# Two RWKV chunks inverted together, with state steps and attention projections woven between them in a written-out TensorE order

## The chip, the cores and the metric

The kernel runs on one core of a Trainium2 chip. A core has TensorE for matrix products, VectorE, ScalarE, GpSimd, and SyncE, which issues transfers. The profile calls them PE (with PEld for the loads of TensorE's weights), DVE, ACT, POOL and SP. The metric is the device time of one execution, in microseconds (us). One execution was also profiled; all rows below are from that one.

## The reference

A trunk of two layers over 528 tokens (16 meta tokens and 512 others) of width 1024. Each layer normalises, makes one projection of 3488 columns, feeds three groups of heads with it (A: RWKV-7, B: differential attention, C: gated linear attention), joins them in an output projection, and ends with 16 experts that each take 66 tokens. What the change touches is group A's recurrence, and the projections of group B that are computed beside it.

```python
def step(S, inp):                       # group A, for each token, both directions
    r_t, w_t, k_t, v_t, kk_t, ka_t = inp
    sa = jnp.einsum("dbhvk,dbhk->dbhv", S, kk_t)
    S = S * w_t[..., None, :] - sa[..., :, None] * ka_t[..., None, :] + v_t[..., :, None] * k_t[..., None, :]
    return S, jnp.einsum("dbhvk,dbhk->dbhv", S, r_t)
...
p = jnp.einsum("bld,dp->blp", u, w_in[l])                 # u: 528 x 1024
q = rotary(q...) * (B_QK_DIM ** -0.5); k = rotary(k...)   # group B, 4 heads
```

## The kernel before

The 528 tokens are padded to nine chunks of 64. For each chunk the recurrence becomes matrix products and one inversion of a unit triangular 64x64 matrix for each of 8 combinations (two directions `d`, four heads; `m` from 0 to 3 counts direction and head pair, `p_` is the half of a pair: partitions 0 to 63 or 64 to 127, given by `hr(p_)`). Step `i` handles chunk `i` of the forward direction and chunk `8 - i` of the backward one.

One step of `rwkv` has two parts.

- **The inversion**, which doesn't need the running state `S`. `pl` (products of `BC` and `az`) is masked into `lt` by VectorE; ScalarE rounds `lt` to half precision (`nh`); VectorE makes `mt` and the first `tz` from it. Five levels follow, each `pq` (TensorE), `vv` (ScalarE), `pz` (TensorE), a subtraction into `tz` and a transpose of it (VectorE). Then `pzt`, `pF`, `pZ` refine the result into `zz`.
- **The state step**: `pbc` and `plv` prepare operands, then `px` from `S`, `xs` on VectorE, `pu` with `zz`, `uv` on ScalarE and VectorE, `pS` and the next `S`, and the output `py` into `Y`.

`az` and `zz` are copies of the operands laid into 128 rows, with zeros in the rows of the other half, so that one product of 128 rows serves both halves.

Ahead of the loop stands `prep`, which makes `AQ`, `BC` and `vt` mainly on VectorE. Behind it in the program stand `heads` (the 12 blocks of 128 columns of group B: projections `pj`, each 48 products of 128x128 weights with 264 columns, 24 for each half of the tokens; then rotary, or a transpose into `vB`), `fin` (normalises `Y`) and `attention` (scores `sm` and `S` at L894 and L904). The program text has the loop first and `heads` next. The order that each engine really gets is decided by the framework's scheduler when the kernel is built, and it mixes the products of `heads` with those of the loop. Engines run their own lists strictly in order and wait for each other by semaphores. `behind(inst, mark)` fixes that `inst` is issued after `mark`, without a wait. PSUM tiles: `rw0` and `rw1` (one each) for the inversion, `sm` (two) for the state step, `mm` (two) for projections.

Of the kernel before, what the change touches and what calls it, by code (L numbers as in the profile page):

```python
# [27 lines left out]
HL = L // 2  # L28
# [38 lines left out]
CST_COLS = _lay([("ident", 128), ("eye", 64), ("ones", 1), ("half", 2), ("ltmask", 512), ("base", 128),  # L67
# [3 lines left out]
def constants():  # L71
# [10 lines left out]
    put("ltmask", np.concatenate([s < t, s < t, s <= t, s <= t, s > t, s > t, s >= t, s >= t], 1))  # L82
# [23 lines left out]
def body(ctx: ExitStack, tc: tile.TileContext, a, out, dbg=None, depth=DEPTH, stop=None):  # L106
# [110 lines left out]
    for l in range(depth):  # L217
# [65 lines left out]
        def proj(blk, M=128):  # L283
            w = wp.tile([128, 1024], F32, name="w")
            nc.sync.dma_start(w, a["w_in"][l, blk])
            wh, wl = split(wp, w, 1024, 2, V if BLK_B <= blk < BLK_C else G)
            p = mm_tile("pj")
            vh = wh.rearrange("p (k m) -> p k m", k=KT)
            vl = wl.rearrange("p (k m) -> p k m", k=KT)
            for c in range(2):  # L290
                n = 0
                for ww, uu in ((vh, uh), (vh, ul), (vl, uh)):
                    for k in range(KT):
                        T.matmul(p[:M, c, :HL], ww[:, k, :M], uu[:, k, c * HL:(c + 1) * HL],  # L294
                                 start=(n == 0), stop=(n == 23))
                        n += 1
            return p[:M, :, :HL]

# [147 lines left out]
        def rwkv(rw):  # L446
            Y = rw.tile([128, 2, NCH, CH], F32, name="Y")
            S = rw.tile([128, 4, CH], F32, name="S", bufs=2)
            G.memset(S, 0.0)
            bc4 = [128, 4, CH]  # L450
            m4 = lambda x: x[:, :256].rearrange("p (m n) -> p m n", m=4)
            MP = [(m, p_) for m in range(4) for p_ in range(2)]
            eyeb = eye[:, None, :].to_broadcast(bc4)
            AZ = [rw.tile([128, 4, 2, 2, CH], F32, name=f"az{x}") for x in range(2)]
            ZZ = [rw.tile([128, 4, 2, CH], F32, name=f"zz{x}") for x in range(1)]
            for p_ in range(2):
                G.memset(ZZ[0][hr(1 - p_), :, p_, :], 0.0)
            for x in range(2):
                for p_ in range(2):
                    G.memset(AZ[x][hr(1 - p_), :, 0, p_, :], 0.0)  # L460
                    G.memset(AZ[x][hr(1 - p_), :, 1, 1 - p_, :], 0.0)
            for i in range(NCH):
                js = (i, NCH - 1 - i)
                jm = [js[m // 2] for m in range(4)]
                az, zz = AZ[i % 2], ZZ[0]
                for d in range(2):
                    for p_ in range(2):
                        for x in range(2):
                            src = AQ[hr(p_), 2 * d:2 * d + 2, js[d], x, :]
                            if x == 0:  # L470
                                A.activation(az[hr(p_), 2 * d:2 * d + 2, 0, p_, :], src, AF.Copy)
                            else:
                                G.tensor_copy(az[hr(p_), 2 * d:2 * d + 2, 1, 1 - p_, :], src)
                lt = rw.tile([128, 2, 512], F32, name="lt", bufs=2).rearrange("p d (b x q n) -> p d b x q n", b=2, x=2, q=2)
                for d in range(2):
                    pl = rw_tile(i, "pl").rearrange("p (b n) -> p b n", b=2)
                    for b in range(2):
                        m = 2 * d + b
                        T.matmul(pl[:, b, :], flat(BC[m][:, jm[m]]), az[:, m].rearrange("p x q n -> p (x q n)"),
                                 start=True, stop=True)  # L480
                    V.tensor_mul(lt[:, d].rearrange("p b x q n -> p b (x q n)"), pl,
                                 ltmask[:, d, None, :].to_broadcast([128, 2, 256]))
                nh = rw.tile(bc4, F16, name="nh", bufs=2)
                nl = rw.tile(bc4, F16, name="nl", bufs=2)
                db = lambda x: x.rearrange("p (d b) n -> p d b n", d=2)
                for p_ in range(2):
                    A.activation(db(nh[hr(p_)]), lt[hr(p_), :, :, 0, p_, :], AF.Copy)
                for p_ in range(2):
                    G.tensor_sub(db(nl[hr(p_)]), lt[hr(p_), :, :, 0, p_, :], db(nh[hr(p_)]))
                mt = rw.tile([128, 5, 4, CH], F16, name="mt", bufs=2)  # L490
                for d in range(2):
                    V.tensor_mul(mt[:, :, 2 * d:2 * d + 2, :],
                                 nh[:, None, 2 * d:2 * d + 2, :].to_broadcast([128, 5, 2, CH]),
                                 lvlm[:, :, d, None, :].to_broadcast([128, 5, 2, CH]))
                tz = rw.tile([128, 2, 4, CH], F16, name="tz", tag=f"tz{i % 2}", bufs=2)
                V.tensor_mul(tz[:, 1].rearrange("p (d b) n -> p d b n", d=2),
                             nh.rearrange("p (d b) n -> p d b n", d=2),
                             basem[:, :, None, :].to_broadcast([128, 2, 2, CH]))
                V.tensor_sub(tz[:, 1], eyeb, tz[:, 1])
# [898 lines left out]
```

## Time and profile before

| | |
|---|---|
| median of three runs | 2705.39 us (2701.43 to 2705.64) |
| profiled execution, its own time | 2698.94 us |
| its span, first to last instruction | 2697.2 us |
| TensorE busy | 2513.8 us (93%) |
| VectorE busy | 2158.7 us (80%) |
| ScalarE busy | 1608.8 us (60%) |
| GpSimd busy | 351.8 us (13%) |
| mean granted TensorE clock, share of full speed | 0.951 |

The two layers run one after the other. The loop of the first layer lies at about 250 to 430 us, that of the second at about 1585 to 1765 us. Each is followed by attention, the output projection and the experts; the experts fill most of the span. A busy TensorE is not a TensorE at its peak: a product's row shows its whole passage through the array, and rows of successive products overlap. The step from the start of one product to the start of the next is what it costs.

### The profile page before, as it was taken

Reading aid. Unit: us, or ns where it says so; the run is one execution under the profiler, and the core shown is the slowest. Engines: PE = TensorE matmul, PEld = TensorE weight load, DVE = VectorE, ACT = ScalarE, POOL = GpSimd, SP = SyncE. Lnnn points to the kernel's source line nnn. Section 1 sums busy time; section 2 is a strip of 40 time slices with the busy share of each in tenths; the row PEclk is TensorE's granted clock in tenths of the full one; section 3 lists DMA queues with packets and bytes.
Section 4 is the critical chain, followed back from the end, with each engine's and each line's share of the span. In section 5 each row is a group of like instructions: output and inputs, shape, how many; then the busy total and the mean of one; then the engine's idle time right before and its main releaser. Section 6 shows DMA issues by size and latency. Waiting matters only on the chain. (4 is left out here: it accounts for less than half of the span.)

```text
span 2697.2 us, 46680 instructions
## 1 busy us (share of the span) xinstructions
PE 2513.8 (93%) x18586; PEld 1983.7 (74%) x18586; DVE 2158.7 (80%) x3389; ACT 1608.8 (60%) x2113; POOL 351.8 (13%) x503
## 2 busy tenths in 40 slices
PE   7889999887999999999788899999699999999995
PEld 6778886666777777778587787756478777777783
DVE  3557677768999999999735666776699999999995
ACT  4324335526888888888542343354178888888884
POOL 3113321001000000000121133210010000000000
PEclk9887999998999999999988889999899999999998
DMA  3101101158999999999420111022499999999993
GB/s 131 48 25 58 39 25 48 64 211 319 403 407 398 410 398 411 399 414 411 174 85 32 40 45 49 14 75 101 150 394 397 411 398 410 400 407 401 413 412 114
DMA packets 84683, 643.30 MB, mean 239 GB/s; under 512 B 12592, under 2 KB 13040, under 8 KB 35312
## 3 DMA queue, kind: packets, MB, share of 16 engines
q1 hardware_dynamic: 75936, 618.16, 57.4%
q0 software_dynamic: 8528, 22.15, 3.3%
q8 instruction: 146, 2.39, 0.4%
q14 instruction: 73, 0.60, 0.1%
HBM read 617.05 MB, written 19.40 MB: 236 GB/s over the span
## 5 line engine op out<-in xcount | busy, mean ns | idle before, releaser
L1159 DVE TENSOR_TENSOR wl<-w,wh 128x1408 fp32r<-128x1408 f32 (+2 forms) x768 | 1212.6, 1617 | 60.4 <-ACT wh L1158 23.5
L1158 ACT ACTIVATE wh<-w 128x1408 fp32r<-128x1408 f32 (+2 forms) x768 | 1042.8, 1378 | 196.5 <-PE py L1267 78.2
L1267 PE MATMUL py<-wh,hh 128*66 128x512 f32 (+1 forms) x768 | 289.0, 376 | 4.3 <-ACT hh L1247 4.3
L1267 PE MATMUL py<-wh,hl 128*66 128x512 f32 (+1 forms) x768 | 288.8, 376 | 0.8 <-DVE hl L1248 0.8
L1267 PE MATMUL py<-wl,hh 128*66 128x512 f32 (+1 forms) x768 | 288.3, 375 | 0.0
L1272 POOL DMA_INDIRECT hbuf<-yo,idx x32 | 54.8, 1713 | 1190.0 <-ACT yo L1271 1076.6
L1206 PE MATMUL h1a<-wh,xx 128*66 128x512 f32 x512 | 185.9, 414 | 1.8 <-DVE xx L1184 1.8
L1206 PE MATMUL h3a<-wh,xx 128*66 128x512 f32 x512 | 182.8, 408 | 0.0
L1206 PE MATMUL h1b<-wh,xx 128*66 128x512 f32 x512 | 175.8, 409 | 0.0
L1206 PE MATMUL h3b<-wh,xx 128*66 128x512 f32 x512 | 174.7, 407 | 0.0
L294 PE MATMUL pj<-uh,wh 128*128 128x264 f32 (+1 forms) x896 | 166.7, 315 | 7.8 <-ACT kS L350 6.5
L1206 PE MATMUL h1T<-xx,wh 128*128 128x132 f32 x768 | 172.0, 224 | 0.0
L1206 PE MATMUL h3T<-xx,wh 128*128 128x132 f32 x768 | 171.3, 223 | 0.0
L294 PE MATMUL pj<-ul,wh 128*128 128x264 f32 (+1 forms) x896 | 162.9, 314 | 0.0
L294 PE MATMUL pj<-uh,wl 128*128 128x264 f32 (+1 forms) x896 | 156.6, 305 | 0.0
L1267 PEld LDWEIGHTS py<-wh,hh 128*66 128x66 f32 x768 | 105.2, 137 | 64.2 <-ACT hh L1247 4.5
L1267 PEld LDWEIGHTS py<-wl,hh 128*66 128x66 f32 x768 | 105.1, 137 | 60.5 <-issue 0.8
L1206 PE MATMUL h1T<-xx,wl 128*128 128x66 f32 x768 | 148.7, 194 | 0.0
L1267 PEld LDWEIGHTS py<-wh,hl 128*66 128x66 f32 x768 | 105.3, 137 | 59.0 <-DVE hl L1248 1.4
L1206 PEld LDWEIGHTS h3T<-xx,wh 128*128 128x128 f32 x768 | 146.6, 191 | 2.7
L1206 PE MATMUL h3T<-xx,wl 128*128 128x66 f32 x768 | 148.3, 193 | 0.0
L1206 PEld LDWEIGHTS h1T<-xx,wh 128*128 128x128 f32 x768 | 148.0, 193 | 0.0
(444 smaller groups left out, 5015.2 us busy)
## 6 DMA issues: line engine op xcount, KB each, us to landing
w<-in_e_w SPq DMA_DIRECT2D x384, 1408.0 KB, 13.6
w<-in_w_in SPq DMA_DIRECT2D x56, 512.0 KB, 3.5
wo<-in_w_out SPq DMA_DIRECT2D x16, 512.0 KB, 3.5
h<-hbuf SPq DMA_DIRECT2D x12, 512.0 KB, 5.2
swp<-raw SPq DMA_DIRECT2D x64, 66.0 KB, 2.0
h<-in_x SPq DMA_DIRECT2D x8, 512.0 KB, 6.9
hbuf<-h SPq DMA_DIRECT2D x8, 512.0 KB, 2.9
ubuf<-u POOLq DMA_DIRECT2D x8, 512.0 KB, 6.1
```

Of the source, the lines that this page charges most:

```text
L294: T.matmul(p[:M, c, :HL], ww[:, k, :M], uu[:, k, c * HL:(c + 1) * HL], start=(n == 0), stop=(n == 23))
L1158: A.activation(wh, w[:, lo:hi], AF.Copy)
L1159: sub = V.tensor_sub(wl, w[:, lo:hi], wh.bitcast(F32))
L1206: T.matmul(o_, l_, r_, start=s0, stop=s1)
L1267: T.matmul(py[:CAP, c, d0:d0 + n], x[:, kk, :], ww[:, at0 - lo:at0 - lo + n], start=(kk == 0 and i_ == 0), stop=(kk == FK - 1 and i_ == 2))
L1272: G.indirect_dma_start(out=hbuf[:, :], out_offset=bass.IndirectOffsetOnAxis(ap=idx[:CAP, e:e + 1], axis=0), in_=yo[:CAP], in_offset=None, ...
```

## The change

What the loop computes stays as it is. It is cut into generators that are advanced by hand.

- `invert(i0, n, res)` inverts two chunks at once (`n` is 2; the ninth chunk is alone). Tiles of the inversion hold 8 matrices instead of 4 for each half of the partitions, so an instruction of VectorE or ScalarE is twice as wide and there are half as many.
- `state(i, ...)` is the state step. `states` runs the two of the pair that was inverted last, while the next pair is inverted.
- `proj_steps` is `proj` with a stop after each 12 products; `heads` becomes a generator; `fill` issues the next 12 products (a burst). There are 48 bursts.
- A loop advances the inversion and the states in turns, with a burst after each turn (first pair, or no state step left) or after each second one. All products that go through `mm` are tied into one chain by `behind`, so TensorE's order is as written.
- `pl`, `px`, `pu` and the first products of `py` take 64 rows of each half directly (`AQ[hr(p_)]`, `S[hr(p_)]`, `zz[hr(p_)]`) instead of 128 rows with zeros. `az` and its copies (four by ScalarE, four by GpSimd for each step) are gone.

```diff
-        def proj(blk, M=128):
+        def proj_steps(blk, M=128):
             w = wp.tile([128, 1024], F32, name="w")
...
+            mm = yield
             for c in range(2):
                 n = 0
                 for ww, uu in ((vh, uh), (vh, ul), (vl, uh)):
                     for k in range(KT):
-                        T.matmul(p[:M, c, :HL], ww[:, k, :M], uu[:, k, c * HL:(c + 1) * HL],
-                                 start=(n == 0), stop=(n == 23))
+                        mm(T.matmul, p[:M, c, :HL], ww[:, k, :M], uu[:, k, c * HL:(c + 1) * HL],
+                           start=(n == 0), stop=(n == 23))
                         n += 1
+                        if n == 12 or (n == 24 and c == 0):
+                            mm = yield
             return p[:M, :, :HL]
...
-        def rwkv(rw):
+        def rwkv(rw, fill):
...
+            def mm(op_, *x, **k):
+                tail[0] = behind(op_(*x, **k), tail[0])
+
+            def burst(n):
+                for _ in range(n):
+                    fill(mm)
...
+            def invert(i0, n, res):
+                QN = 4 * n
...
+                lt = rw.tile([128, 2, 8, 2, CH], F32, name="lt", bufs=2)
+                for d in range(2):
+                    pls = [rw_tile(p_, "pl") for p_ in range(2)]
+                    for q, i, m in Q[2 * n * d:2 * n * (d + 1)]:
+                        for p_ in range(2):
+                            o_ = (q - 2 * n * d) * 128
+                            mm(T.matmul, pls[p_][:, o_:o_ + 128], flat(BC[m][hr(p_), at(i, m)]),
+                               flat(AQ[hr(p_), m, at(i, m)]), start=True, stop=True)
+                    for p_ in range(2):
+                        V.tensor_mul(lt[:, p_, dq(d)].rearrange("p q x n -> p q (x n)"),
...
+                    if d == 0:
+                        yield
+                yield
...
                 for v in range(5):
-                    pq = m4(rw_tile(i, "pq"))
-                    for m, p_ in MP:
-                        T.matmul(pq[hr(p_), m, :], mt[hr(p_), v, m, :], tz[hr(p_), 0, m, :], start=True, stop=True)
...
+                    pq = mq(rw_tile(0, "pq"))
+                    for q, p_ in QP:
+                        mm(T.matmul, pq[hr(p_), q], mt[hr(p_), v, q], tz[hr(p_), 0, q], start=True, stop=True)
+                    vv = tile_("vv")
                     A.activation(vv, pq, AF.Copy)
...
+                    yield
+                    pz = mq(rw_tile(1, "pz"))
...
-                for m in range(4):
-                    T.matmul(px[:, m, :], flat(az[:, m, 0]), S[:, m, :], start=True, stop=True)
+                for m, p_ in MP:
+                    mm(T.matmul, px[hr(p_), m, :], AQ[hr(p_), m, at(i, m), 0, :], S[hr(p_), m, :], start=True, stop=True)
...
+            ready = []
+            for i0 in range(0, NCH + 2, 2):
+                res = []
+                inv = invert(i0, min(2, NCH - i0), res) if i0 < NCH else iter(())
+                st = states(ready)
+                going, step = [inv, st], 0
+                while going:
+                    for g in (inv, st):
+                        if g in going:
+                            try:
+                                next(g)
+                            except StopIteration:
+                                going.remove(g)
+                    if i0 == 0 or step % 2 or st not in going:
+                        burst(1)
+                    step += 1
+                ready = res
```

A burst of the changed program is "pj ... x8" and "pj ... x4" in the listings of order that follow. Products that go through `mm` all carry line L467, whatever they compute.

The first place is TensorE's list at the end of `prep`, before the first `pq`. In the listing of before, the last `up` of `prep` (L313) is followed by projections in long stretches.

```order
L313 MATMUL up<-ad,wa 128x264 x2
L294 MATMUL pj<-uh,wh 128x264 x8
L294 MATMUL pj<-ul,wh 128x264 x8
L294 MATMUL pj<-uh,wl 128x264 x8
L479 MATMUL pl<-az_2117,bc_282 128x256
L479 MATMUL pl<-az_2118,bc_282 128x256
L294 MATMUL pj<-uh,wh 128x264 x8
L294 MATMUL pj<-ul,wh 128x264 x8
L294 MATMUL pj<-uh,wl 128x264 x8
L294 MATMUL pj<-uh,wh 128x264 x2
```

In the changed program the same place reads as follows (`bc_282` to `bc_285` are `BC` of `m` 0 to 3; the last row is the weight load of the first `pq`).

```order
L327 MATMUL up<-ad,wa 128x264 x2
L467 MATMUL pl<-aq,bc_283 128x128 x2
L467 MATMUL pl<-aq,bc_282 128x128 x2
L467 MATMUL pl<-aq,bc_283 128x128 x2
L467 MATMUL pj<-uh,wh 128x264 x8
L467 MATMUL pj<-ul,wh 128x264 x4
L467 MATMUL pl<-aq,bc_284 128x128 x2
...
L467 MATMUL pj<-ul,wh 128x264 x3
L455 MATMUL pb<-cst,ta 64x1 x18
L467 MATMUL pj<-ul,wh 128x264
L467 MATMUL pj<-uh,wl 128x264 x8
L467 LDWEIGHTS mt
```

Two bursts (24 projections) now stand between `prep` and the first `pq`, and each waits its turn behind `pl`; the others have moved into the loop.

The second place is TensorE's list at the start of a later pair: the second half of `pl`, the first state step's `px`, one burst, and the first `pq` of the new pair.

```order
L467 MATMUL plv<-vt,lt 64x64 x8
L467 MATMUL pl<-aq,bc_284 128x128 x2
L467 MATMUL pl<-aq,bc_285 128x128 x2
L467 MATMUL pl<-aq,bc_284 128x128 x2
L467 MATMUL pl<-aq,bc_285 128x128 x2
L467 MATMUL px<-S,aq 64x64 x8
L467 MATMUL pj<-uh,wh 128x264 x8
L467 MATMUL pj<-ul,wh 128x264 x4
L467 LDWEIGHTS mt
```

The third place is VectorE's list in the same stretch of the third pair: from the masking of `pl` to the first `uv`.

```order
L493 TENSOR_TENSOR lt<-pl,hst 128x512 x4
L825 TENSOR_TENSOR raw<-raw,rot 128x528
L581 TENSOR_TENSOR xs<-px,lv 128x256
L833 TENSOR_TENSOR k_3295<-raw,swp 64x528 x2
L507 TENSOR_TENSOR tz<-nh,hst 128x256 x2
L513 TENSOR_TENSOR mt<-nh,hst 128x5x256
L508 TENSOR_TENSOR tz<-cst,tz 128x512
L513 TENSOR_TENSOR mt<-nh,hst 128x5x256
L510 STREAM_TRANSPOSE tz<-tz 128x256 x2
L587 TENSOR_SCALAR uv<-pu 64x4x64
```

Between the last `lt` and the first `pq` VectorE now has this whole list to go through, at double width; `raw` and `k` are rotary work of `heads`, and stand there in the third pair only. Before, VectorE's list alternated between two chunks at different levels:

```order
L553 TENSOR_TENSOR xs<-px,lv 128x256
L511 TENSOR_TENSOR tz<-tz,pz 128x256
L481 TENSOR_TENSOR lt<-pl,hst 128x512
L526 TENSOR_TENSOR g_3035<-g_3035,pF 128x256
L481 TENSOR_TENSOR lt<-pl,hst 128x512
L531 TENSOR_TENSOR zz_2119<-zt,pZ 64x4x64 x2
L492 TENSOR_TENSOR mt<-nh,hst 128x5x128 x2
L496 TENSOR_TENSOR tz<-nh,hst 128x256
```

There, levels of the other chunk stood between the steps that open a chunk; now each pair is opened in one piece.

## Rows read from the trace of the kernel before

**Rows 1.** Windows of the first layer: busy us, count, clock, DMA share, GB/s.

```profile
core 0: us, PE busy (x) PEld busy (x) DVE busy (x) ACT busy (x) POOL busy (x), PEclk, DMA share, GB/s
350.00:400.00 50.00, 49.35 (x630) 39.79 (x629) 35.07 (x76) 17.68 (x42) 14.40 (x30) 1.00 0.06 18
...
428.00:435.00 7.00, 6.72 (x62) 5.01 (x61) 5.37 (x30) 4.04 (x8) 1.90 (x3) 1.00 0.43 150
435.00:500.00 65.00, 56.91 (x328) 33.22 (x324) 56.42 (x209) 39.70 (x122) 6.38 (x10) 0.95 0.17 59
500.00:535.00 35.00, 33.54 (x183) 24.33 (x182) 28.05 (x112) 20.42 (x68) 0.00 (x0) 1.00 0.12 42
```

**Rows 2.** Timeline of PE at the loop's start: start us, us, what.

```profile
249.20 0.68 PE L544 MATMUL plv<-vt,lt 64*64 64x64 f32 x16
249.81 0.51 PE L294 MATMUL pj<-uh,wh 128*128 128x264 f32 x2
250.16 1.00 PE L551 MATMUL px<-S,az 128*128 128x64 f32 x8
250.97 0.98 PE L294 MATMUL pj<-uh,wh 128*128 128x264 f32 x6
251.79 1.14 PE L294 MATMUL pj<-ul,wh 128*128 128x264 f32 x8
252.76 0.40 PE L294 MATMUL pj<-uh,wl 128*128 128x264 f32 x2
253.09 0.31 PE L504 MATMUL pq<-tz,mt 64*64 64x64 f16 x8
253.34 0.75 PE L294 MATMUL pj<-uh,wl 128*128 128x264 f32 x4
254.01 0.31 PE L509 MATMUL pz<-vv,tz 64*64 64x64 f16 x8
```

**Rows 3.** Timeline of PE at the loop's end.

```profile
425.52 0.43 PE L569 MATMUL py<-S,az 128*128 128x64 f32 x2
...
426.15 0.43 PE L569 MATMUL py<-S,az 128*128 128x64 f32 x2
...
427.15 0.34 PE L571 MATMUL py<-uv,lt 128*64 128x64 f32 x4
...
427.74 0.51 PE L294 MATMUL pj<-uh,wh 128*128 128x264 f32 x2
```

**Rows 4.** Groups of PE, 250 to 430 us: busy us, mean ns, idle before.

```profile
L479 PE MATMUL pl<-az,bc 128*128 128x256 f32 x56 | 17.7, 403 | 0.0
```

**Rows 5.** Groups of DVE, 250 to 430 us.

```profile
L492 DVE TENSOR_TENSOR mt<-nh,hst 128x640 f16<-128x640 f16 x16 | 10.0, 651 | 2.2 <-ACT nh L487 2.2
L481 DVE TENSOR_TENSOR lt<-pl,hst 128x512 f32<-128x512 f32 x14 | 9.6, 685 | 2.3 <-PE pl L479 2.3
L772 DVE TENSOR_TENSOR raw<-raw,rot 128x528 f32<-128x528 f32 x8 | 7.4, 927 | 0.0
L499 DVE TENSOR_TENSOR tz<-cst,tz 128x256 f16<-128x256 f32 x9 | 4.2, 464 | 0.2
L500 DVE STREAM_TRANSPOSE tz<-tz 128x256 f16<-128x256 f16 x9 | 4.0, 441 | 0.2
L496 DVE TENSOR_TENSOR tz<-nh,hst 128x256 f16<-128x256 f16 x8 | 4.0, 494 | 0.0
```

**Rows 6.** Groups of ACT, 250 to 430 us.

```profile
L506 ACT ACTIVATE vv<-pq 128x256 f16<-128x256 f32 x45 | 17.2, 382 | 39.0 <-PE pq L504 38.4
L537 ACT ACTIVATE bct<-pbc 128x512 f32<-128x512 f32 x8 | 4.8, 597 | 5.4 <-PE pbc L535 5.1
```

**Rows 7.** Windows with a granted clock that falls, both layers.

```profile
196.50:199.90 3.40, 0.20 (x2) 0.00 (x0) 3.27 (x6) 0.43 (x2) 0.22 (x2) 1.00 0.05 19
199.90:213.60 13.70, 13.05 (x84) 12.68 (x84) 6.91 (x10) 3.28 (x5) 0.33 (x4) 0.50 0.12 39
...
1582.30:1589.10 6.80, 6.80 (x43) 6.38 (x40) 3.88 (x10) 3.34 (x10) 6.37 (x13) 0.50 0.27 65
```

More of the change, by code (lines that the diff above doesn't have):

```diff
@@ L511, in rwkv @@
+                    tn = rw.tile([128, 2, 8, CH], F16, name="tz", bufs=2)[:, :, :QN]
                     V.tensor_sub(tn[:, 0], tz[:, 0], pz)
                     if v < 4:
-                        V.transpose(flat(tn[:, 1]), flat(tn[:, 0]))
+                        for q in range(0, QN, 4):
+                            V.transpose(flat(tn[:, 1, q:q + 4]), flat(tn[:, 0, q:q + 4]))
                     tz = tn
-                pzt = rw_tile(i, "pzt", F16)[:, :256].rearrange("p (m n) -> p m n", m=4)
@@ L516, in rwkv @@
-                for m, p_ in MP:
-                    T.transpose(pzt[hr(p_), m, :], tz[hr(p_), 0, m, :], ident16[hr(p_), hr(p_)])
-                zt = rw.tile(bc4, F16, name="zt", bufs=2)
+                    yield
+                pzt = mq(rw_tile(0, "pzt", F16))
+                for q, p_ in QP:
+                    mm(T.transpose, pzt[hr(p_), q], tz[hr(p_), 0, q], ident16[hr(p_), hr(p_)])
+                zt = tile_("zt", "vv")
                 A.activation(zt, pzt, AF.Copy)
-                g1 = rw.tile(bc4, F16, name="g1", bufs=2)
+                g1 = tile_("g1")
@@ L533, in rwkv, with state @@
+                zz = rw.tile([128, 8, CH], F32, name="zz", bufs=2)
+                V.tensor_add(zz[:, :QN], zt, pZ)
+                for c in range(n):
+                    res.append((i0 + c, lt, zz, [2 * n * (m // 2) + 2 * c + m % 2 for m in range(4)]))
+            Ss = [rw.tile([128, 4, CH], F32, name="S", bufs=2)]
+            G.memset(Ss[0], 0.0)
+            bc4 = [128, 4, CH]
+            def state(i, lt, zz, qs):
+                js = (i, NCH - 1 - i)
+                S = Ss[-1]
                 pbc = sm_tile("pbc").rearrange("p (m n) -> p m n", m=4)
@@ L764, in heads @@
                 for h in range(4):
-                    p = proj(BLK_B + 4 * which + h)
+                    p = yield from proj_steps(BLK_B + 4 * which + h)
                     raw = at.tile([128, 528], F32, name="raw", tag="tb", bufs=4)[:, :L]
@@ L790, in heads @@
                 raw = at.tile([128, 528], F32, name="raw", tag="tb", bufs=4)[:, :L]
-                A.activation(two(raw), proj(BLK_B + 8 + h), AF.Copy)
+                p = yield from proj_steps(BLK_B + 8 + h)
+                A.activation(two(raw), p, AF.Copy)
                 pt = sm_tile("pt")
@@ L950, in body, with fill @@
             rp = rwp.enter_context(tc.tile_pool(name="rw", bufs=1, side="left", reuse_waits="tile"))
-            Y = rwkv(rp)
-        if "a" in order:
             ap_ = parts.enter_context(tc.tile_pool(name="at", bufs=1, side="right", reuse_waits="tile"))
-            hd = heads(ap_)
+            steps, done = heads(ap_), []
+            next(steps)
+            def fill(mm):
+                try:
+                    if not done:
+                        steps.send(mm)
+                except StopIteration as end:
+                    done.append(end.value)
+            Y = rwkv(rp, fill)
+            while not done:
+                fill(lambda op_, *x, **k: op_(*x, **k))
+            hd = done[0]
         if "r" in order:
```

150 lines of the change are left out of this document (69 added, 81 removed).

## The prediction

> **What bounds the kernel now.** I read the windows first, to see which engine is full in the stage that the change touches. Between 350 and 400 us, inside the loop of the first layer, TensorE is busy 49.35 of 50 us at full clock, VectorE 35.07, ScalarE 17.68 [rows 1]. The groups of ScalarE say the same from the other side: it stood idle 38.4 us ahead of `vv`, waiting for `pq` [rows 6]. So the loop is a TensorE stage: a wait in one chunk's chain costs nothing, since the scheduler has another chunk or a projection to put there. Behind the loop that turns round. From 435 to 535 us VectorE is busy 84.5 of 100 us, against 35.07 of 50 in the loop [rows 1].
>
> Then the timeline of TensorE, for what a product costs there. Inside a stretch of projections eight take 0.97 us (251.79 to 252.76), 0.121 us each; a stretch of four between small products takes 0.67 us (253.34 to 254.01) [rows 2]. Four at 0.121 would be 0.48, so going into projections and out again costs 0.19 us. Between 252 and 428 us there are 111 such stretches, the first at 251.79 [rows 2], the last at 427.74 [rows 3]. 20 us of a full engine are spent on changing over.
>
> **The change, part by part.** I take one layer, from the first `pq`, at 253.1 us [rows 2], to the end of the last `py`, at 427.5 [rows 3]: 174.4 us.
>
> *Bursts.* 48 bursts less the two that stand ahead of the first `pq` leave 46 stretches where 111 were: 65 x 0.19 = 12.4 us saved.
>
> *64-row tiles.* `px` now takes 0.81 us (250.16 to 250.97) for 8 instructions of 128 rows and 128 weights; `plv`, already made of 64-row halves, needs 0.61 us for 16 [rows 2]. I price the new `px` and `pu` at that row: 2 x 0.20 saved per step, `pu` taken like `px`. `py` alternates between both kinds, 0.63 us for each of four (425.52 to 426.15) [rows 3], 2.52 per step; as two uniform groups it should be 2 x 0.61 to 0.70, say 1.31. Together 1.61 us, times nine steps 14.5 us.
>
> *`pl`.* Same number of columns, but its two halves may run side by side. Seven steps cost 17.7 us of busy time [rows 4]. Bounds: nothing saved, if the halves wait for each other; 8.8, if they overlap fully. `plv` overlaps, but with 64 weights, not 128; I take 4.
>
> *Groups of 16.* `pq`, `pz`, `pzt` and `pZ` stood in groups of 8 at 0.25 us (253.09 to 253.34) [rows 2]. A group of 16 costs between 0.25 and 0.50, as changing over is a part of it that I can't separate here; I take the middle, 0.38. 48 groups of 16 for 96 of 8: 24.0 - 18.2 = 5.8 us, bounds 0 and 12.
>
> *Work moved in.* The list of before puts 114 projections between the last `up` and the first `pq`, in time in which TensorE has little else; the new list has 24. The other 90 come into the loop: 90 x 0.121 = 10.9 us back.
>
> TensorE's work in the loop: 174.4 - 12.4 - 14.5 - 4 - 5.8 + 10.9 = 148.6 us.
>
> *What comes back as waits.* TensorE's order is now fixed, and it waits wherever the next product isn't ready. The worst place is the opening of a pair. Between the second half of `pl` and the first `pq` VectorE and ScalarE go through: two `lt` at 0.685; one `nh` of 512 columns, 0.60 like `bct` [rows 6]; two `tz` at 0.494; two `mt` of double width; one subtraction of double width; two transposes at 0.441 [rows 5]. `mt` lies between 0.65 (no dearer for its width) and 1.30; the subtraction between 0.46 and 0.93. Four handoffs at 0.11 (`pq` ends at 253.40, `vv` takes 0.38, `pz` starts at 254.01: 0.23 for two [rows 2, 6]). That makes 6.0 to 7.8 us, 7.1 by my choice near the wide ends, as instructions of 512 columns already cost about what their width says. In this time TensorE has `px` (0.61) and one burst (12 x 0.121 + 0.19 = 1.65): 2.3 us. It stands idle 3.8 to 5.6 us; I take 4.8, three times: 14.4. Queued behind that `pq` are `pu` and so the state step. The first pair has this wait too, but there it takes the place of the end of `prep`, and its first `pq` comes when the first `pq` came before, within 1.5 us. In the third pair `raw` (0.93) and two `k` (0.70 each, taken like the 0.685 row) stand in VectorE's list ahead of `tz`, partly behind `nh`: 1.9 us more.
>
> Inside a pair the waits are small: a burst (1.65) covers `vv` (0.6 and two handoffs); a state product covers most of it. Per pair I count 0.3 us where the second half of `pl` waits for PSUM that `lt` frees, and 0.25 twice where `pz` follows `pu`: 0.8, three times 2.4 us.
>
> The ninth chunk has four bursts and then none; the last state step stands alone. Of three bare levels each leaves about 1.1 us open, the opening at half width 1.6, the end (`zz`, `xs`, `uv`) about 3, less what attention's scores fill: 7 us, between 4 and 10.
>
> *The clock.* After 3.2 us without products the granted clock was 0.50 for 13.7 us; in the second layer it was 0.50 for 6.8 us in the middle of the loop's opening, with TensorE busy throughout [rows 7]. A wait of 4.8 us is like the first. I charge 3 us to the first pair, which begins cold, and 1.5 us to each of three others, since part of the slow stretch falls into the wait: 7.5 us, bounds 2 and 24 (three times half of 13.7, and 3).
>
> Waits: 14.4 + 1.9 + 2.4 + 7 + 7.5 = 33.2 us. Loop: 148.6 + 33.2 = 181.8, against 174.4: 7.4 us longer.
>
> *Copies taken out.* `az` on ScalarE and GpSimd saves nothing: both have idle time, 32 of 50 us on ScalarE [rows 1].
>
> *Behind the loop.* From 428 to 535 us VectorE does 5.37 + 56.42 + 28.05 = 89.8 us of work [rows 1]. In the new list 39 of its instructions of `fin` and `attention` stand ahead of the last `Y`, in the old one 19; at 56.42 / 209 = 0.27 us [rows 1] that is 5.4 us done earlier. The rest, 84.4 us, at the pace of 84.5 in 100, takes 100 us instead of 107: 7 us back.
>
> Sum for a layer: +7.4 - 7 = +0.4 us. In the second layer the 6.8 us at half clock lie ahead of the first `pq` with TensorE as the limit; in the new list it has only two bursts there: 3 us less. Both layers: 0.8 - 3 = -2.2 us. The profiled execution took 2698.94 us by its own time, which gives 2696.7; the median is 6.45 us above it, so 2703 us is what I expect of the median.
>
> **Where a rule speaks against it.** `plv` shows products of two row halves, written into one PSUM tile, at 0.61 us for 16, less than `px` needs for 8 [rows 2]. The Trainium skill, "TensorEngine Tiling (Array Packing)", Restrictions and Gotchas, says that different row tiles cannot use the same PSUM bank at the same time. By that rule `px`, `pu` and the first half of `py`, which write both halves into one tile, would not overlap; the trace disagrees for `plv`, which has the same form. As a rival it is kept below, with the price of `px`.
>
> **The rivals.**
>
> *The openings are covered better (2672 us, faster).* If `mt` and the subtraction cost little more than now, the idle time is 3.8 us instead of 4.8; if `pl` overlaps fully, 4.8 us more are saved; if the clock stays up, 4.5; the end 3 us less. 15 us a layer, 30 in all. For it: all of these are lower bounds of rows. Against it: they are independent, and `mt` at 651 ns already stands for a mean with other work beside it.
>
> *The clock falls after each opening (2738 us, slower).* If each of the three openings, and that of the ninth chunk, is followed by 13.7 us at half speed as at 199.9 us [rows 7], each costs 6 us where I charged 1.5: 4.5 x 3 + 4 = 17.5 a layer, 35 in all. It decides from the point at which a slow stretch lasts over about 5 us beyond the wait. Against it: the state steps and the bursts that follow keep TensorE nearly full.
>
> *Row halves don't overlap (2760 us, slower).* 16 instructions at 0.81 / 8 instead of 0.61 / 16: 1.6 us for each of `px`, `pu` and half of `py`, 1.0 x 3 x 9 = 27 a layer. `plv` speaks against it.
>
> *VectorE holds the levels up (2725 us, slower).* Its list has `raw`, `wl` and `q` or `k` between a subtraction and its transposes; where one of them waits for a transfer, the level waits. 0.5 us on each of 23 levels is 11 a layer. For it: the order is strict; against it: bursts leave 1.65 us at each half level.
>
> **How the numbers follow.** The forecast gets 0.43, the first rival 0.25, the clock 0.18, the row halves 0.04, VectorE 0.10. 2703 is the likeliest; its own range, from the choices within the bounds, is 2686 to 2720. A measurement of this kernel can tell about 0.2% (5.4 us) from no change, so faster means below 2700.0 and slower above 2710.8. The forecast splits 0.17, 0.18, 0.08 over faster, same and slower. With the rivals: faster 0.42, same 0.18, slower 0.40. The range for 8 in 10 leaves 0.08 below and 0.12 above: 2664 to 2746.
>
> **What would show it.** In the profile after: stretches of 12 projections of about 1.65 us; `px` and `pu` at 0.6 us; three idle times of 4 to 5 us in each layer ahead of the first `pq` of a pair, ended by a transpose on VectorE; TensorE idle ahead of the first pair, where projections stood; the last `py` of the first layer near 435 us and the last `norm` near where it was. The clock row shows whether the loop stays at 1.00. The prediction is wrong if the idle time at the openings is below 3 us, if the clock is low for most of a pair, or if the time of a level is set by VectorE and not by bursts.

## The result and the profile after

The changed kernel takes 2737.67 us, median of 4 runs (2732.82 to 2742.61), the kernel before 2703.41: ratio 1.0133, 95% interval 1.0106 to 1.016. It is slower by 1.3%. The profiled execution took 2741.48 us (span 2739.7), 42.5 us more than that of before. By the end of its last output projection the first layer is 23.2 us later (614.55 for 591.37 us), and the second adds 19.0 us.

The loop of layer 1 and what lies behind it up to that projection, in windows (columns as in [rows 1]), of the kernel before and then of the changed one:

```profile
253.09:427.48 174.39, 172.07 (x2150) 139.71 (x2150) 114.98 (x248) 60.11 (x144) 53.65 (x109) 1.00 0.13 40
427.48:591.40 163.92, 154.06 (x868) 104.69 (x867) 120.09 (x463) 72.54 (x213) 9.95 (x15) 0.98 0.27 99
```

```profile
254.38:457.21 202.83, 174.42 (x2616) 150.35 (x2618) 119.83 (x229) 60.69 (x124) 45.40 (x69) 0.89 0.12 36
457.21:614.50 157.29, 143.03 (x791) 96.82 (x791) 113.63 (x439) 64.25 (x185) 7.66 (x14) 0.97 0.30 106
```

The loop takes 202.8 us instead of 174.4. TensorE is about as long busy as before (174.4 us for 172.1), but at a mean granted clock of 0.89, and it stands still for 28.4 us. Where the clock went is in windows cut at its changes, which answer to [rows 7]; 0.50 is 1.2 GHz, 1.00 is 2.4:

```profile
298.20:332.30 34.10, 30.59 (x512) 27.26 (x512) 22.57 (x35) 11.83 (x22) 9.65 (x14) 1.00 0.24 72
332.30:346.00 13.70, 8.58 (x108) 7.74 (x108) 7.88 (x15) 1.42 (x4) 2.63 (x5) 0.50 0.00 1
346.00:380.10 34.10, 28.28 (x469) 24.87 (x468) 19.80 (x32) 10.04 (x18) 9.37 (x9) 1.00 0.17 48
380.10:390.30 10.20, 8.18 (x107) 7.54 (x108) 4.95 (x12) 2.31 (x4) 1.16 (x4) 0.50 0.01 2
390.30:424.50 34.20, 30.86 (x507) 26.35 (x505) 16.35 (x36) 10.98 (x21) 5.43 (x16) 1.00 0.01 3
424.50:431.30 6.80, 6.35 (x66) 5.79 (x66) 3.97 (x12) 0.00 (x0) 1.17 (x4) 0.50 0.01 2
```

Each of these slow stretches begins at the opening of a pair or of the ninth chunk, and lasts on while TensorE is busy again; others lie at the first pair (up to 260.6) and the second (3.4 us each from 287.9 and from 294.8). The opening of the third pair on the timeline of TensorE (start us, us, what, idle before):

```profile
326.41 1.40 PE L467 MATMUL pl<-aq,bc 64*128 64x128 f32 x16
327.74 0.68 PE L467 MATMUL px<-S,aq 64*64 64x64 f32 x16
328.35 1.23 PE L467 MATMUL pj<-uh,wh 128*128 128x264 f32 x8
329.42 0.65 PE L467 MATMUL pj<-ul,wh 128*128 128x264 f32 x4
337.32 0.75 PE L467 MATMUL pq<-tz,mt 64*64 64x64 f16 x16 [7.25 <-DVE tz L510]
337.82 1.14 PE L467 MATMUL pu<-xs,zz 64*64 64x64 f32 x16
338.81 0.64 PE L467 MATMUL pz<-vv,tz 64*64 64x64 f16 x16
339.53 1.54 PE L467 MATMUL pS<-uv,bct 128*64 128x64 f32 x16
341.00 1.12 PE L467 MATMUL py<-S,aq 64*64 64x64 f32 x16
342.05 1.12 PE L467 MATMUL py<-uv,lt 128*64 128x64 f32 x16
```

`px` goes by in 0.61 us (327.74 to 328.35) and a burst in 1.72 (328.35 to 330.07), then nothing for 7.25 us, and `pu`, which waits for nothing else, stands behind that `pq`. After it a group of 16 `py` takes 1.05 us (341.00 to 342.05) where `px` took 0.61: half the clock. What VectorE and GpSimd did in those 7.25 us (timelines of both):

```profile
331.11 3.21 DVE L833 TENSOR_TENSOR k<-raw,swp 64x528 f32<-64x528 f32 x2 [0.86 <-POOL swp L824]
334.34 0.49 DVE L507 TENSOR_TENSOR tz<-nh,hst 128x256 f16<-128x256 f16 x2
334.75 0.82 DVE L513 TENSOR_TENSOR mt<-nh,hst 128x1280 f16<-128x1280 f16 x1
335.49 0.68 DVE L508 TENSOR_TENSOR tz<-cst,tz 128x512 f16<-128x512 f32 x1
336.09 0.82 DVE L513 TENSOR_TENSOR mt<-nh,hst 128x1280 f16<-128x1280 f16 x1
336.82 0.76 DVE L510 STREAM_TRANSPOSE tz<-tz 128x256 f16<-128x256 f16 x2
```

```profile
331.04 2.73 POOL L504 TENSOR_TENSOR nl<-lt,nh 64x512 f16<-64x512 f32 x2
```

VectorE first waited for a rotary `swp`, then two `k` took 3.21 us beside GpSimd's `nl`, and only then came `tz`, with both `mt` ahead of the transposes.

For all kernels below I count TensorE's time from the first `pq` to the last `py` of layer 1 in three parts, from its records: standing still (gaps between records), lost to the clock (half of the busy time that lies at 0.50), and the rest, work at full clock. Before: 172.1 work, 0 clock, 2.3 still. After: 156.4, 18.1 and 28.4.

Two groups of TensorE's work in that window did not stand there before, the scores of attention and the transposes of its values:

```profile
L958 PE MATMUL S<-k,q 128*128 128x512 f32 x10 | 5.6, 642 | 0.0
L851 PE MATMUL pt<-cst,raw 128*128 128x128 f32 x16 | 2.6, 286 | 0.0
```

With `sm`, `pg`, `pf` and the other `pt` such products come to 10.9 us at full clock, counted from start to next start.

### The profile page after: what moved, and what is told of

Its sections match the earlier page's. It is cut to its first block, busy times and chain, and to the rows that moved or that the text cites. A ratio compares the mean times of both kernels' runs of the same rounds, so it can differ in the third digit from the quotient of the medians.

```text
span 2739.7 us, 47449 instructions
## 1 busy us (share of the span) xinstructions
PE 2478.9 (90%) x19162; PEld 1968.8 (72%) x19162; DVE 2150.0 (78%) x3297; ACT 1578.5 (58%) x1977; POOL 316.2 (12%) x387
## 5 line engine op out<-in xcount | busy, mean ns | idle before, releaser
L1271 PE MATMUL h1T<-xx,wh 128*128 128x132 f32 x768 | 172.1, 224 | 0.0
L1271 PEld LDWEIGHTS h1T<-xx,wl 128*128 128x128 f32 x768 | 146.0, 190 | 0.0
L1271 PEld LDWEIGHTS h3T<-xx,wl 128*128 128x128 f32 x768 | 144.7, 188 | 0.0
L208 ACT ACTIVATE wh<-w 128x1024 fp32r<-128x1024 f32 x56 | 59.2, 1058 | 144.4 <-PE pj L302 52.2
```

Of the source, the lines that this page charges most:

```text
L208: A.activation(wh[:, :n], w[:, :n], AF.Copy)
L1271: T.matmul(o_, l_, r_, start=s0, stop=s1)
```

## The experiments

Two theories. **A**: the order by hand leaves TensorE standing at the openings, and the clock falls behind each wait; the new shapes and bursts are worth what they were priced at. **B**: the time is set by VectorE's longer chain of a pair (or by the shapes), and order and clock only show it. The runs, with first `pq` to last `py` of layer 1 ("loop") and its three parts, and from there to the last output projection ("behind"). Each ratio is to runs of the kernel before taken beside that run, with medians of 2699.7 to 2703.4 us:

| kernel | median us | ratio to before, 95% | loop | work | clock | still | behind |
|---|---|---|---|---|---|---|---|
| before | 2703.4 | | 174.4 | 172.1 | 0.0 | 2.3 | 163.9 |
| changed | 2737.7 | 1.0106 to 1.0160 | 202.8 | 156.4 | 18.1 | 28.4 | 157.3 |
| 64-row px, pu, py alone | 2662.0 | 0.9823 to 0.9882 | 146.2 | 142.9 | 0.0 | 3.4 | 170.3 |
| free order | 2673.7 | 0.9875 to 0.9926 | 165.6 | 150.5 | 6.4 | 8.7 | 158.6 |
| products added | 2721.6 | 1.0043 to 1.0087 | 191.4 | 173.7 | 4.8 | 12.9 | 157.6 |
| shorter opening | 2715.9 | 1.0034 to 1.0065 | 194.4 | 157.5 | 13.2 | 23.7 | 157.7 |
| woven anew | 2678.5 | 0.9900 to 0.9933 | 172.0 | 151.3 | 5.1 | 15.6 | 152.5 |
| free order, shorter opening | 2668.5 | 0.9859 to 0.9904 | 166.6 | 154.9 | 2.8 | 8.8 | 158.0 |
| scores behind the loop | 2735.7 | 1.0110 to 1.0144 | 199.6 | 150.6 | 16.0 | 33.1 | 159.2 |
| pl in halves, one chunk | 2782.5 | 1.0278 to 1.0314 | 218.1 | 150.5 | 28.5 | 39.2 | 160.7 |
| nl later | 2718.8 | 1.0054 to 1.0088 | 192.2 | 158.0 | 10.1 | 24.1 | 155.7 |
| free, shorter, nl later | 2654.2 | 0.9814 to 0.9847 | 162.6 | 155.0 | 1.7 | 6.0 | 157.7 |
| woven anew, nl later | 2663.6 | 0.9852 to 0.9886 | 167.9 | 151.2 | 2.5 | 14.1 | 152.3 |

**The 64-row products alone.** From the kernel before:

```diff
-                for m in range(4):
-                    T.matmul(px[:, m, :], flat(az[:, m, 0]), S[:, m, :], start=True, stop=True)
+                for m, p_ in MP:
+                    T.matmul(px[hr(p_), m, :], AQ[hr(p_), m, jm[m], 0, :], S[hr(p_), m, :], start=True, stop=True)
...
```

> The kernel before with one part of the change alone: px, pu and py as 64-row products (8, 8 and 16 instructions in place of 4, 4 and 12), VectorE's zz in one 128-row operation; one chunk at a time, the old pl, the order still the scheduler's. Theory A (the forecast's term for these products is right and TensorE sets the pace of the loop): 14.5 us less TensorE work per layer, so first pq to last py 158 to 162 us in layer 1 (174.4 before), about 28 us off the whole, 2675 us. Rival B (products of the two row halves that write one PSUM tile go one after the other, so nothing is saved): 2700 to 2710 us. Rival C (the work falls but the chain of one chunk's inversion then sets the pace): TensorE's work falls by 14 us and waits rise by as much, 2695 to 2705 us.

A, and more than expected. The timeline of TensorE:

```profile
318.86 0.68 PE L566 MATMUL py<-S,aq 64*64 64x64 f32 x16
319.47 0.69 PE L569 MATMUL py<-uv,lt 128*64 128x64 f32 x16
...
322.27 0.68 PE L548 MATMUL px<-S,aq 64*64 64x64 f32 x16 [0.29 <-ACT bct L534]
322.88 0.70 PE L477 MATMUL pl<-az,bc 128*128 128x256 f32 x2
```

0.61 us for 16 instructions, as `plv` in [rows 2], where 8 of 128 rows took 0.81 for the same result (the trace has two instructions for each of these fp32 products, 288 `plv` for 144 in the program). The loop ends 28 us sooner, but part of that is that it holds 368 projections instead of 444: the rest went behind it, which got 6.4 us longer. Together 21.8 us per layer, out of 19.8 us less work. Where the scheduler fills TensorE's waits, work saved is time saved.

**The order left to the scheduler.** From the changed kernel:

```diff
             def mm(op_, *x, **k):
-                tail[0] = behind(op_(*x, **k), tail[0])
+                op_(*x, **k)
```

> The changed kernel with one part undone: the ties that fix TensorE's order in the loop are gone, so the scheduler places the same products (pairs of chunks, groups of 16, 64-row products, bursts in steps of 12 all kept in the code). Theory A (the loss is the hand-written order: nothing else may run at the five openings, and prep's end is left empty): the waits ahead of first pq groups fall from 18.6 us to under 8 us in layer 1, the stretches at 1.2 GHz with them, loop 175 to 185 us, whole 2685 to 2705 us. Rival B (the loss is the pair's longer opening chain on VectorE and ScalarE, which no order of TensorE covers): loop 198 to 206 us, whole 2730 to 2745 us.

A, with loop and whole (165.6 and 2673.7 us) below the ranges expected. The third pair's opening:

```profile
312.37 0.88 PE L467 MATMUL pj<-uh,wl 128*128 128x264 f32 x5
313.08 1.13 PE L467 MATMUL pj<-uh,wh 128*128 128x264 f32 x8
314.05 1.14 PE L467 MATMUL pj<-ul,wh 128*128 128x264 f32 x8
315.02 0.40 PE L467 MATMUL pj<-uh,wl 128*128 128x264 f32 x2
316.58 0.31 PE L467 MATMUL pq<-tz,mt 64*64 64x64 f16 x8 [1.15 <-DVE tz L510]
```

23 projections stand where the changed kernel stood still for 7.25 us. The loop is 37 us shorter, of which 5.9 us are work: only 450 projections are in it instead of 552, since the others fill the end of `prep` again.

**Products added.** Products that nothing reads, and nothing taken out:

```diff
+            def idle(n):
+                p = sm_tile("id")
+                for _ in range(n):
+                    mm(T.matmul, p[:, :HL], uh[:, 0, :128], uh[:, 1, :HL], start=True, stop=True)
...
+                    if step == 1 and i0 < NCH:
+                        idle({0: 16, 2: 24, 4: 44, 6: 36, 8: 18}[i0])
```

> The changed kernel with work added and nothing else: at each pair's opening, behind the burst, 16, 24, 44, 36 and 18 further 128x128 by 264 products into a spare PSUM tile that nothing reads (0.14 us each at 2.4 GHz, 19 us per layer in all), so that TensorE is busy where it stands still now. Theory A (the drop to 1.2 GHz that follows each opening's wait costs 18 us per layer by itself): the stretches at 1.2 GHz in the loop shrink to under 12 us of time, loop 192 to 198 us in layer 1, whole 2718 to 2730 us although work is added. Rival B (the slow stretches lie where TensorE has slack and cost little; only the waits count): the added products fill waits and overrun some, loop 203 to 210 us, whole 2738 to 2755 us.

A. The third opening, and a window over most of the loop:

```profile
320.59 5.48 PE L467 MATMUL id<-uh 128*128 128x264 f32 x44
327.25 0.64 PE L467 MATMUL pq<-tz,mt 64*64 64x64 f16 x16 [1.17 <-DVE tz L515]
```

```profile
282.70:426.00 143.30, 133.59 (x2141) 117.86 (x2141) 90.33 (x171) 42.46 (x82) 34.30 (x59) 1.00 0.10 30
```

138 such products a layer, 122 of them, 15.2 us, in the loop, and the loop is 11.4 us shorter. The waits it fills would by themselves have given nothing: still 28.4 to 12.9 is 15.5 us, as much as the added work (other products took 2.2 us more). What is gained is the clock, 18.1 to 4.8: 13.3 us that the slow clock cost in one layer by itself.

**A shorter opening.** `nh`, `tz` and the transpose by direction; the first level's `mt` apart:

```diff
+                    V.tensor_sub(tz[:, 1, dq(d)], eyeb[:, :2 * n], tz[:, 1, dq(d)])
+                    V.tensor_mul(mt0[:, dq(d)], nh[:, dq(d)], lvlm[:, 0, d, None, :].to_broadcast([128, 2 * n, CH]))
+                    dv = V.transpose(flat(tz[:, 0, dq(d)]), flat(tz[:, 1, dq(d)]))
+                for d in range(2):
+                    behind(V.tensor_mul(mt[:, :, dq(d)], nh[:, None, dq(d)].to_broadcast([128, 4, 2 * n, CH]),
+                                        lvlm[:, 1:, d, None, :].to_broadcast([128, 4, 2 * n, CH])), dv)
```

> The changed kernel with a shorter opening: nh, the base of tz and its transpose are made by direction, the first direction while pl of the second runs, and mt of the first level has a tile of its own (two 128x256 operations), so that the other four levels' mt (two 128x1024) come behind the transposes instead of ahead of them. TensorE's order and work stay. From the end of the first direction's lt to the first pq: 8.0 us now at the second pair, by the trace's durations 5.5 to 6. Theory A (the openings' waits and the slow clock behind them are what is lost): 2 us less at each of the five openings and a third to a half of the slow stretches gone, loop 185 to 194 us in layer 1, whole 2700 to 2722 us. Rival B (VectorE is the bound behind the opening, so the time moves to the next level's wait): loop 199 to 204 us, whole 2730 to 2742 us.

A in size of the whole; the loop lies at the edge. At the second pair the wait did not get shorter (2.58 us for 2.48), and VectorE's timeline says why:

```profile
287.15 0.75 DVE L506 TENSOR_TENSOR tz<-nh,hst 128x256 f16<-128x256 f16 x1
287.82 0.28 DVE L508 TENSOR_TENSOR mt<-nh,hst 128x256 f16<-128x256 f16 x1
288.02 1.37 DVE L507 TENSOR_TENSOR tz<-cst,tz 128x256 f16<-128x256 f32 x1
289.43 0.45 DVE L509 STREAM_TRANSPOSE tz<-tz 128x256 f16<-128x256 f16 x1
```

The subtraction took 1.37 us here and 0.42 for the first direction, and the first `tz` 0.75 for 0.29. In that time, from 286.60 to 289.11 us, GpSimd ran `nl`.

**nl later.** So `nl` was moved, in the changed kernel, to the fourth level; `pF` is the first to read it:

```diff
-                for p_ in range(2):
-                    G.tensor_sub(nl[hr(p_)], lt[hr(p_), p_, :QN, 0, :], nh[hr(p_)])
...
-                    A.activation(vv, pq, AF.Copy)
+                    mark = A.activation(vv, pq, AF.Copy)
+                    if v == 3:
+                        for p_ in range(2):
+                            after(G.tensor_sub(nl[hr(p_)], lt[hr(p_), p_, :QN, 0, :], nh[hr(p_)]), mark)
```

> The changed kernel with GpSimd's two nl moved: they wait for vv of the fourth level instead of following nh, so that GpSimd is idle while VectorE goes through an opening (nl isn't read before pF). In the changed kernel two k took 3.21 us on VectorE while nl ran beside them in the third opening (one alone 0.70), and mt 1.78 against 0.82 in the second. Theory A (GpSimd's nl holds VectorE up in the opening): the waits ahead of the first pq groups are 1 to 2 us shorter each, with part of the slow clock behind them, loop 190 to 197 us in layer 1, whole 2715 to 2730 us. Rival B (VectorE's long instructions there have another cause, or nl costs as much where it now runs): loop 200 to 205 us, whole 2732 to 2742 us.

A, though the second pair's wait is no shorter (2.62 us for 2.48): the five waits ahead of a first `pq` come to 13.7 us for 18.6. Groups of VectorE in the loop (busy us, mean ns), of the changed kernel and then of this run:

```profile
L833 DVE TENSOR_TENSOR k<-raw,swp 64x528 f32<-64x528 f32 x8 | 7.4, 927 | 3.4 <-POOL swp L824 3.3
L513 DVE TENSOR_TENSOR mt<-nh,hst 128x1280 f16<-128x1280 f16 x6 | 6.8, 1135 | 0.0
L507 DVE TENSOR_TENSOR tz<-nh,hst 128x256 f16<-128x256 f16 x6 | 2.3, 424 | 0.6 <-ACT nh L502 0.5
```

```profile
L834 DVE TENSOR_TENSOR k<-raw,swp 64x528 f32<-64x528 f32 x8 | 5.6, 702 | 1.5 <-POOL swp L825 1.2
L511 DVE TENSOR_TENSOR mt<-nh,hst 128x1280 f16<-128x1280 f16 x6 | 4.9, 819 | 0.0
L505 DVE TENSOR_TENSOR tz<-nh,hst 128x256 f16<-128x256 f16 x6 | 1.5, 290 | 1.0 <-ACT nh L502 1.0
```

The same instructions are a quarter to a third shorter when GpSimd's `nl` isn't beside them, and the kernel falls from 1.0133 to 1.0071 of before: two instructions per pair, on an engine with idle time. The Trainium skill, "SBUF — State Buffer", Terms, says that VectorE and GpSimd share a pair of ports to SBUF, of which the loser is blocked for the other's whole instruction; the trace agrees (`k` 702 ns apart from `nl`, 927 on average with it beside some of them).

Taken one by one, the instructions of the changed kernel's loop show it more sharply than the means: six of the eight `k` took 0.70 to 0.71 us, and the two with `nl` beside them 1.63 and 1.57. `raw` shows that the one that starts first keeps its pace: six that started no later than GpSimd's `swp` took 0.71 us, and the `swp` then 1.83 to 1.88; two that started behind it took 1.48 and 1.53, and the `swp` 1.30 and 1.32. With `nl` moved, four of the eight `raw` started behind `swp`, and the mean of all eight rose from 906 to 1172 ns, so VectorE lost a part of what it had gained.

**Woven anew.** On the shorter opening, in steps of 6 projections, by a list of letters (I a step of the inversion, S one of the state, b six projections):

```diff
+            first = "bbbbbbbbbI bbbbbbI bbbbI bI bbI bI bbI bI bbI bI bbI bI bbI bbI b"
+            pair = "ISb ISbbbSb IS Ibb SIS Ibb IS Ibb IS Ibb IS Ibb Ibb Ib"
+            last = "IS ISbbbSb IS Ib SIS Ib IS I IS I IS I I I"
```

> The run with the shorter opening, woven anew: the same products, TensorE's order still fixed by hand, but projections in steps of 6, nineteen of them ahead of the first pq (nine ahead of pl, six between its halves, four behind), four behind px and pu in each later opening, one behind pq and two behind pz while the first pair is alone, and behind pz alone in the later pairs, where a state product follows pq. Theory A (a fixed order is no loss by itself; the loss is where it leaves TensorE standing): first pq still at 253 to 256 us, waits ahead of first pq groups under 6 us together, under 10 us of TensorE's busy time at 1.2 GHz in the loop, loop 150 to 160 us in layer 1, whole 2635 to 2660 us, below both the kernel before and the run with a free order. Rival B (with the openings filled, VectorE's chain of a level sets the pace, whatever the order): waits of about 1 us at each level, loop 165 to 175 us, whole 2675 to 2700 us.

Between the two. The openings' waits shrank (1.69 us at the second, 0.46 at the third), and what the clock costs with them (5.1 us), so a fixed order can beat the kernel before; but loop and whole came out in B's range, with 15.6 us still standing behind VectorE and ScalarE.

> The run woven anew, with nl moved in the same way. Its waits (15.6 us in the loop of layer 1) end on VectorE's and ScalarE's tz, uv and vv. Theory A: the waits at and right behind the openings (1.7 us at the second, 1.2 at pS and 2.2 at pz of the third) go by half and more, loop 166 to 169 us, whole 2662 to 2672 us. Rival B (VectorE is late for its own load of 124 of 172 us): loop 170 to 173 us, whole 2675 to 2682 us.

A for the whole and the loop. Of the waits that A named, that of the second opening fell to 0.75 us and that at `pS` is gone, but that at `pz` in the third pair grew from 2.2 us to 3.17, the longest that is left:

```profile
343.12 0.75 PE L467 MATMUL pz<-vv,tz 64*64 64x64 f16 x16 [3.17 <-DVE tz L531]
```

```profile
341.12 1.47 DVE L834 TENSOR_TENSOR k<-raw,swp 64x528 f32<-64x528 f32 x2 [1.66 <-POOL swp L825]
342.62 0.77 DVE L531 STREAM_TRANSPOSE tz<-tz 128x256 f16<-128x256 f16 x2
```

VectorE's list had `k` ahead of the transposes, `k` waited for GpSimd's `swp`, and a level of the inversion waited for both.

**Free order with the shorter opening, and with nl later.** Both edits on the run with the free order:

> The run with the free order and the run with the shorter opening together. Theory A (where the scheduler may put other products into the opening, its length costs little): within 6 us of the free order alone, 2668 to 2679 us. Rival B (the opening's chain is what each pair waits for in any order): 2 us less for each of ten openings, 2650 to 2660 us.

A: 2668.5 us, and its ratio, 0.9881, lies within the free order's own interval.

> The run with the free order and the shorter opening, with nl moved behind the fourth level's vv in the same way. Theory A: VectorE's chain still sets some of the waits there (8.8 us idle in the loop of layer 1), 1 to 4 us less a layer, 2660 to 2667 us. Rival B (the scheduler has other products for these waits): 2665 to 2674 us.

Better than A: 2654.2 us, 1.7% below the kernel before, the lowest median of all runs; its interval overlaps that of the 64-row products alone, so the two aren't told apart.

**Scores behind the loop.** One tie more in the changed kernel: the first scores follow the last `py`.

```diff
-            hd = done[0]
+            hd = done[0][:4] + (last,)
```

> The changed kernel with one tie more: attention's first score products (S and sm, 6.2 us of TensorE in the loop of layer 1) may not run before the last py of the loop. Theory A (they are work that only moved: what they cost in the loop they save behind it): loop 195 to 199 us in layer 1 (202.8 in the changed kernel), the part behind it longer by as much, whole 2730 to 2744 us. Rival B (they hold the loop up and are free behind it): loop 195 to 199 us, whole 2720 to 2728 us. Rival C (they only fill waits of the last chunks): loop 201 to 204 us, whole 2742 to 2755 us.

A, nearly: the loop gets 3.2 us shorter (5.8 us of work out and 2.1 less lost to the clock, 4.7 more standing still), what is behind it 1.9 longer, and the whole stays. They are work that moved, and most of it had lain in waits.

**pl in halves, one chunk at a time.** From the 64-row run:

```diff
+                pls = [rw_tile(i, "pl"), sm_tile("pl")]
+                for m in range(4):
+                    for p_ in range(2):
+                        T.matmul(pls[p_][:, m * 128:m * 128 + 128], flat(BC[m][hr(p_), jm[m]]), flat(AQ[hr(p_), m, jm[m]]),
+                                 start=True, stop=True)
```

> The run with px, pu and py in 64-row halves (one chunk at a time, the scheduler's order), and pl in 64-row halves too: 8 products of 64 rows and 128 columns straight from aq, each half in a PSUM tile of its own (the second one of the tag sm), in place of 8 of 128 rows and 256 columns, so that az and its copies on ScalarE and GpSimd go. Theory A (work taken off TensorE is worth its time wherever the scheduler can fill its waits): pl of the loop 9 us in place of 14.9 (64 products of 64 x 128 took 9.1 in the changed kernel), 5 to 7 us off each layer, whole 2645 to 2655 us, the fastest of all runs. Rival B (the second PSUM tile is taken from the state steps, whose chain then waits): 2658 to 2675 us.

Rival B, and far beyond its range. TensorE late in the loop:

```profile
405.28 0.31 PE L490 MATMUL pq<-tz,mt 64*64 64x64 f16 x8 [2.17 <-DVE tz L486]
406.07 0.31 PE L495 MATMUL pz<-vv,tz 64*64 64x64 f16 x8 [0.47 <-ACT vv L492]
406.89 0.42 PE L490 MATMUL pq<-tz,mt 64*64 64x64 f16 x8 [0.51 <-DVE tz L497]
407.84 0.42 PE L495 MATMUL pz<-vv,tz 64*64 64x64 f16 x8 [0.53 <-ACT vv L492]
```

The next chunk's `pl` takes its second tile from those of the state steps, in program order behind the last chunk's, so two chunks no longer overlap: each chunk's `pl` starts within 1 us of the `pu` of the chunk before, or behind its `py`, and its 40 `pq` stand alone between two `pu` (306.3 to 315.7, 331.1 to 341.0 us), while in the 64-row run the first 80, those of two chunks, lie ahead of the first `pu`. The projections fill the gaps until the last of them at 378.1 us; from there on a chunk's bare chain is what one sees, mostly at 1.2 GHz.

## Why the prediction was wrong

It gave 2703 us, a loop 7.4 us longer and 7 us less behind it. Measured in layer 1: 28.4 longer and 6.6 less. The step that failed is the price of the clock behind the openings, 7.5 us for 18.1; beside it one kind of work that moved into the loop was not in the sum at all.

- *TensorE's work*, 148.6 us predicted: right for the loop's own products, 145.4 (156.4 less the 10.9 of attention and `fin`). By parts, saved: `px`, `pu` and `py` 17.6 us (38.86 to 21.22) for 14.5; `pl` 4.0 for 4 (1.30 us for a chunk, 1.86 before, seven chunks); groups of 16 5.6 for 5.8. A projection costs 0.138 us instead of 0.171, and a burst 1.65 (261.50 to 263.15, in the first pair), as priced. The first `pq` came 1.3 us later, within the 1.5.
- *Work moved in* lacked a term: it counted projections only (90; 108 more are in the loop) and not the 10.9 us of products of attention and `fin`. It had seen their VectorE side, as the 7 us back behind the loop, and booked the gain without the cost. How much of the 10.9 is a cost is only in part shown: the run that holds the scores back takes 5.8 us of it out, but 4.7 of that turn into waits; its loop gets 3.2 shorter, what is behind 1.9 longer, and the whole stays.
- *The clock* is the step that failed: 7.5 us charged, 18.1 measured, and the run with added products shows 13.3 of it to be a cost by itself. The 3 us of the first pair were right (3.1). The next three pairs were charged 1.5 each and lost 3.4, 4.3 and 4.1; the ninth chunk was charged nothing and lost 3.2. The forecast held that state steps and bursts, which keep TensorE nearly full, would shorten the slow stretches. They didn't: at the third and fourth pair the clock stayed at 0.50 for 8.7 and 8.3 us beyond the first `pq` (337.32 to 346.0, 381.96 to 390.3), and at the ninth chunk it fell only behind the first `pq` (422.73) and stayed low from 424.5 to 431.3. The rival's point of decision was 5 us, and its mechanism is what happened. That its time (2738) was met as well is in part luck: it added 17.5 us a layer for the clock, where the clock's part of the miss is 10.6.
- *Openings*, 16.3 us for three pairs with the third's 1.9: the waits were 2.48, 7.25 and 3.99, 13.7 together. Near in sum, but partly by luck, and the second lies below the 3 us that the forecast named as a sign of being wrong: a part of the second was covered by TensorE's own slow clock (its burst took 2.62 us, 289.33 to 291.95), and the third cost 7.25 for 6.7 with `swp` ahead of `k` and `nl` beside it, a contention that the prediction didn't have (5.12 with `nl` moved). All waits: 28.4 for 25.7.
- So the miss of 21.0 us in the loop (202.8 for 181.8) is, by TensorE's records, 10.6 from the clock, 10.9 from the products of attention and `fin` and 2.7 from waits, less 3.2 of work saved beyond the sum. This adds up the time; it doesn't say what each would bring if it alone were taken away.
- *Behind the loop* the forecast held: VectorE's work there fell by 6.5 us (120.09 to 113.63; 5.4 forecast), and the time by 6.6.
- *The second layer* was to gain 3 us ahead of its first `pq`. Counted from the first layer's last output projection, that `pq` came 2.5 us later instead (999.7 us for 997.1); no run shows why. Its loop is 22.7 us longer (198.1 for 175.4), with 16.7 us lost to the clock for 0.3.
- *Row halves don't overlap* is out: 16 instructions into one PSUM tile in 0.61 us. The sentence of the Trainium skill that the prediction names, "TensorEngine Tiling (Array Packing)", Restrictions and Gotchas, doesn't hold for this form: half rows into their own half of the partitions.
- *VectorE holds the levels up* was small in the changed kernel (2.5 us of waits for `tz` ahead of later `pq`); in the version woven anew most of the waits that are left end on VectorE.

The range, 2664 to 2746, held the time. What the forecast didn't ask is what the change is worth in parts: over loop and behind together, in the same three parts, TensorE's work falls by 27 us in layer 1 (322.9 to 295.8), the projections moved in already counted, and waits and clock go from 15.4 to 64.3. The free order has 289.6 and 34.6; with the opening shortened and `nl` moved, it has 294.1 and 26.2. The 64-row `px`, `pu` and `py` alone have 303.2 and 13.4. So the rest of the change (pairs, `pl` in halves, bursts) takes 13.6 us more off TensorE in the free order and gives 21.2 back in waits and clock: on top of the 64-row products it brought no time that these runs can tell, with the order free (ratio 0.9901 against 0.9853) or with all that was mended (0.9831).

## What to carry to other kernels

A fixed order is to be costed by its waits twice, once for the wait and once for the clock behind it; where TensorE must wait, any product put there, even a useless one, can pay. When work changes sides of a boundary, book it on both sides and on every engine. And a short instruction on an idle engine may lengthen those beside it: look for the same form of instruction with two durations.

## What the runs showed of the hardware

- Behind the first pair, four waits of 1.69 to 7.25 us ahead of a first `pq` came with 6.8 to 13.7 us each at 1.2 GHz, most of it with TensorE busy (at the second pair in two stretches, the first of which began 1.5 us after a wait of 1.29 us for `lt`). With unread products in the waits, 44 of them in the longest, 1.17 us of that one was left, and the clock stayed at 2.4 GHz from 282.7 to 426 us.
- VectorE's `k`, `mt` and `tz`, with both inputs in SBUF, took 702, 819 and 290 ns, and 927, 1135 and 424 on average where GpSimd's `nl` ran beside some of them; in the worst place two `k` took 3.21 us. `raw` took 0.71 us where it started no later than GpSimd's `swp`, and 1.48 and 1.53 where it started behind it.
- Instructions of the two row halves went by at 0.038 us each (64 by 64 by 64 in fp32, two instructions for a product) when each wrote its own half of the partitions of one PSUM tile, where instructions of 128 rows took 0.101: they did not wait for one another.
